# Attention scores with the low part of q against the high part of k alone, as two 64-row products, and the last head's query tiles in reverse order

## The chip, the cores and the metric

The kernel runs on one core of one Trainium2 chip. The metric is the device time of one execution in microseconds. A core has a matrix engine (TensorE, PE in the rows, with its weight loads as PEld), VectorE (DVE), ScalarE (ACT), GpSimd (POOL) and SyncE (SP), which issues the DMAs.

## The reference, cut to what matters

A decoder block over 16 learned meta tokens and 1024 positions of width 1024: a differential-attention branch and a gated-linear-attention branch, merged by gates, with a residual and an RMSNorm at the end. The change concerns the differential attention: 8 heads, each with two maps of head size 64.

```
def probs(q, k):
    s = einsum("bhqd,bhkd->bhqk", q, k) * 64 ** -0.5
    return softmax(where(k_pos <= q_pos, s, -inf))
p   = probs(q1, k1) - lam * probs(q2, k2)
o_a = einsum("bhqk,bhkv->bhqv", p, v)      # then RMSNorm, silu gate, w_branch_a
```

All is float32. The kernel splits each operand into a high part (the type fp32r, which the matrix engine takes in one pass) and a low part, the rest, and sums the products of the parts.

## The kernel before

The kernel runs in stages: normalise and transpose x, project it (a Strassen form for most weights), the linear-attention heads, then the attention stage, branch a, and the output projection. In every stage a small planner (class `Schedule`) is given operations with an engine, an estimated time, dependencies, buffers ("rings") and priorities. It simulates them once and so writes out a fixed order for each engine; on the chip an engine takes its instructions in that order.

In the attention stage a head has eight query tiles `t` of 128 rows, and each tile two maps `j`. A score tile `i` is one (tile, map). Query tile `qt` sees `nk` = 16 + 128 (`qt` + 1) keys, the meta keys first. The operands stand so that the parts are joined by the contraction over 128 rows: `q[:, 0]` holds the high part of q twice (rows 0 to 63 and 64 to 127), `q[:, 1]` the low part twice, and the tile `kk` the high part of k in rows 0 to 63 and the low part in rows 64 to 127. So `qh` times `kk` is high times high plus high times low (L1738), and `ql` times `kk` is low times high plus low times low (L1739). Then a product of an identity with a bf16 mask is added on the diagonal block (L1741). Tiles with `nk` over 512 are cut into two pieces of equal width in two PSUM banks; for `qt` 7 the 16 meta keys are done apart (L1750, L1751). Two score tiles fit at a time (ring "S", two buffers of two banks).

After a score tile come: the max on VectorE (L1767), the exp on ScalarE with its sum (L1779), for both maps the reciprocal (L1787), the scaling of the second map on GpSimd (L1791) and the combination on VectorE (L1796). For each pair `n` of query tiles `value(n)` transposes the combined p (L1852; the meta keys at L1831), splits it and multiplies it with v (L1873 for meta, L1879 to L1881), one pair after the other; then the norm (L1903), the gate (L1918, L1919), a split into high and low (L1935, L1939) and, except for the last head, a store to DRAM. The last head's results go into the place of a tile that branch b reads.

In the gaps PE gets the remaining v projection (L453 to L455) and branch b (L2021 to L2023 into `ps_y`). Branch a, the same lines into `ps_s`, follows and takes the banks of the scores.

The loads of `kk`, q (two halves of four query tiles, one buffer each), v (`va`, `vb`, one buffer each) and meta v (`vm`, three DMAs) are in SP's order. Those of heads 0 and 1 that come at the beginning are issued by `early(i)` of the stage before, in this order: k and first q half of head 0, second q half, k of head 1, v and meta v of head 0. `kk` has two buffers, so head h + 2 is loaded when head h has its last scores.

For the rows of other places: L427 to L429 are projection products, L564 and L589 those of the Strassen form, L1359 a product in the linear-attention heads over the 16 meta rows with plain F32 operands, which PE runs as two pieces, and L1511 a like one over 128 rows.

Of the kernel before, what the change touches and what calls it, by code (L numbers as in the profile page):

```python
# [10 lines left out]
F32 = mybir.dt.float32  # L11
# [9 lines left out]
P = 128  # L21
D = 1024
KC = D // P
NM = 16
# [141 lines left out]
def tile_hybrid_block(  # L166
# [1500 lines left out]
    with ExitStack() as es:  # L1667
# [26 lines left out]
        def load_q(h, hf):  # L1694
            def run():
                for j in range(2):
                    load_qj(A["pool"] if hf else sq, h, hf, j)

            loads["q", h, hf] = op("SP", 3.0 if h else 0.0, run if h else lambda: None, take=f"q{hf}", lat=3.0,
                                   prio=16 * h + 8 * hf)  # L1700

        def load_v(h):
            for i, (k, us) in enumerate((("va", 1.5), ("vb", 1.5), ("vm", 0.5))):
                run = (lambda i=i: load_vp(h, i)) if h else lambda: None
                st = tuple(vst[h // 2]) if h // 2 >= VA else ()
                loads[k, h] = op("SP", us if h else 0.0, run, st, take=k, lat=3.0, prio=16 * h + (8 if i == 1 else 4))
# [3 lines left out]
        step, stat = {}, {}  # L1710
# [5 lines left out]

        def scores(i):
            h, qt, j = i // 16, i % 16 // 2, i % 2
            nk = n_of(i // 2)
            big = nk > 1024  # L1720
            qh, ql, kk = qk(h, j, qt)
            sc = psS.tile([P, 2, 512], F32, name="ps_s", tag="s")
            extra = None
            if nk <= 512:
                pieces = [(0, nk, sc[:, 0, :nk])]
                k0, n, ps = 0, nk, sc[:, 0, :nk]
            elif not big:
                hn = nk // 2
                pieces = [(0, hn, sc[:, 0, :hn]), (hn, hn, sc[:, 1, :hn])]
                k0, n, ps = 0, nk, sc[:, :, :hn]  # L1730
            else:
                extra = tiles["mk", h][:, j]
                pieces = [(NM, 512, sc[:, 0]), (NM + 512, 512, sc[:, 1])]
                k0, n, ps = NM, 1024, sc[:, :, :]
            diag = nk - P
# [6 lines left out]
            step[i] = (k0, n, ps, extra)  # L1742

        def meta_scores(h):

            ms = psY.tile([P, 512], F32, name="ps_ms", tag="misc")[:, : 2 * NM]
            for j in range(2):
                qh, ql, kk = qk(h, j, 7)
                d = ms[:, NM * j : NM * (j + 1)]
                mm(d, qh, kk[:, :NM], start=True, stop=False)  # L1750
                mm(d, ql, kk[:, :NM], start=False, stop=True)  # L1751
            tiles["ms", h] = ms
# [18 lines left out]
        def expo(i):  # L1771
            k0, n, ps, extra = step.pop(i)
            t, j = i // 2, i % 2
            b = stat[t]["nm"][:, j : j + 1]
            pt = tiles["p", t, j] = s3.tile([P, T], F32, name=f"p{j}", tag=f"p{j}", bufs=sch.rings[f"p{j}"])
            dst = pt[:, k0 : k0 + n]
            if len(ps.shape) == 3:
                dst = dst.rearrange("p (a b) -> p a b", a=2)
            act(dst, ps, AF.Exp, bias=b, accum_out=stat[t]["sm"][:, j : j + 1])  # L1779
            if extra is not None:  # L1780
                act(pt[:, :NM], extra, AF.Exp, bias=b, accum_out=stat[t]["sm2"][:, j : j + 1])
# [7 lines left out]
        def second(t):  # L1789
            p2 = tiles["p", t, 1][:, : n_of(t)]  # L1790
            nc.gpsimd.tensor_scalar(p2, p2, stat[t]["r"][:, 1:2], nlam, ALU.mult, ALU.mult)  # L1791

        def both(t):

            p1, p2 = (tiles["p", t, j][:, : n_of(t)] for j in range(2))
            stt(p1, p1, stat[t]["r"][:, 0:1], p2, ALU.mult, ALU.add)  # L1796
            del stat[t], tiles["p", t, 1]

        def softmax(t):
            h, qt = t // 8, t % 8  # L1800
            nk = n_of(t)
            if qt == 7:
                ms = op("PE", 0.4, lambda: meta_scores(h), (S_[2 * t - 1],), take="misc", prio=2 * t - 3)
                mk = op("ACT", 0.09, lambda: meta_copy(h), (ms,), take="mk", use=(("misc", ms),), prio=2 * t - 3)
            for j in range(2):
# [3 lines left out]
                deps = (q, kk) + ((S_[i - 1],) if i else ()) + ((mk,) if qt == 7 else ())  # L1809
# [3 lines left out]
                M_[i] = op("DVE", dm, lambda i=i: vmax(i), (S_[i],) + ((mk,) if qt == 7 else ()),  # L1813
                           take="" if j else "sm", use=(("mk", mk),) if qt == 7 else (), prio=i + PR["M"])
                de = nk * 0.84e-3 + 0.23 + (0.3 if qt == 7 else 0)
                E_[i] = op("ACT", de, lambda i=i: expo(i), (M_[i],) + ((E_[i - 1],) if i else ()), take=f"p{j}",
                           use=(("S", S_[i]),) + ((("mk", mk),) if qt == 7 else ()), prio=i + PR["E"])
            b = 2 * t + 1
# [9 lines left out]
        def meta_t(n):  # L1828
            pv = psY.tile([P, 512], F32, name="ps_pm", tag="misc")[:NM, :256]
            for qi in range(2):  # L1830
                nc.tensor.transpose(pv[:, P * qi : P * (qi + 1)], tiles["p", 2 * n + qi, 0][:, :NM], ident)  # L1831
            val[n]["mv"] = pv

        def meta_hi(n):
            pm = val[n]["pm"] = pms[n % 2]
# [7 lines left out]
        def trans(n, b):  # L1843
            tp = psT.tile([P, 512], F32, name="ps_t", tag="t")
            blocks, o = [], 0
            for kb in (2 * b, 2 * b + 1):
                o0 = o
                for qi in range(2):
                    if kb > 2 * (n % 4) + qi:
                        continue  # L1850
                    p = tiles["p", 2 * n + qi, 0][:, NM + P * kb : NM + P * (kb + 1)]
# [69 lines left out]
        def out_parts(n):  # L1921
# [6 lines left out]
            if pq == 0:  # L1928
# [20 lines left out]
        def value(n):  # L1949
            h, pq = n // 4, n % 4  # L1950
            t0 = 4 * n + 3
# [7 lines left out]
            for b in range(pq + 1):  # L1959
# [9 lines left out]
                          (tl, v) + ((ml, vm) if first else (last,)) + ((A_[n - 1],) if first and n else ()),  # L1969
# [20 lines left out]
            else:  # L1990
                hi = op("ACT", 0.27, lambda: out_split_hi(n), (gt, *oops["b", h]) + tuple(oa_last[:1]), take="" if pq else f"o{h}",
# [33 lines left out]
        def branch(kind, i, order, bank, take, evac, w):  # L2025
# [4 lines left out]
            for n, (k, c) in enumerate(order):  # L2030
# [11 lines left out]
                prev = op("PE", mm3(512), run, (w["ops"][k // 4],) + src_deps(kind, k, c) + ((prev,) if prev else ()), take=t,  # L2042
# [48 lines left out]
        for t in range(8 * H):  # L2091
            softmax(t)
            if t % 2:
                value(t // 2)
# [50 lines left out]
        for i in range(KC):  # L2145
# [4 lines left out]
            ends = branch("a", i, order, bank_s if i < KC - 1 else bank_1, "S", evac_a, w)  # L2150
# [416 lines left out]
```

## Time and profile before

| | |
|---|---|
| median of 3 runs | 1374.7 us (1372.65 to 1375.21) |
| the profiled execution | 1372.48 us, span 1370.7 us |
| granted TensorE clock, mean | 0.995 |
| TensorE busy | 1320.3 us (96%), weight loads 1153.7 us (84%) |
| VectorE, ScalarE, GpSimd busy | 875.6, 748.7, 591.0 us |
| attention stage | about 861 to 1170 us |

The times of the trace count from the span's start. Matmuls overlap in their pipeline, so that their durations add up to more than the time they take; the distance from one to the next, or from end to end, says what one costs. Idle time is put down to what ended it ("<-"), "issue" being idle time for which the profile shows no wait.

### The profile page before, as it was taken

How to read it: one execution, taken by the hardware profiler on the slowest of the kernel's cores; microseconds unless marked ns; L12 is line 12 of the kernel's file. 1: busy time of each engine (PE TensorE's matmuls, PEld its weight loads, DVE VectorE, ACT ScalarE, POOL GpSimd, SP SyncE). 2: the span in 40 equal slices, each digit the busy share in tenths (PEclk: the TensorE clock that was granted, in tenths of full speed). 3: DMA queues.
4: the chain of work that ended last, by engine and by line, in shares of the span. 5: the costliest groups of instructions: out<-in, count | busy, mean ns of one | idle time of the engine just before them, and what ended most of it. 6: DMA issues, size and time to landing. Idle time of an engine off the chain costs nothing.

```text
span 1370.7 us, 22183 instructions
## 1 busy us (share of the span) xinstructions
PE 1320.3 (96%) x7736; PEld 1153.7 (84%) x7736; DVE 875.6 (64%) x1456; ACT 748.7 (55%) x1639; POOL 591.0 (43%) x598
## 2 busy tenths in 40 slices
PE   6999999999999999999999999899999999999897
PEld 5988889889888888888999999788888888778686
DVE  5845464555555444458778885677777778366874
ACT  7643332553566665664546554577777677321433
POOL 4113232452445323215455454447676665443534
PEclk9999999999999999999999999999999999999999
DMA  6226473324433333284734583788765653787232
GB/s 225 90 70 200 137 248 117 108 85 126 131 123 103 106 115 115 93 252 145 218 97 140 185 281 109 231 296 273 252 217 185 205 186 116 259 289 261 93 123 85
DMA packets 133696, 229.22 MB, mean 167 GB/s; under 512 B 14273, under 2 KB 60673, under 8 KB 133585
## 3 DMA queue, kind: packets, MB, share of 16 engines
q1 hardware_dynamic: 133216, 226.50, 50.0%
q0 software_dynamic: 368, 1.31, 0.3%
q8 instruction: 61, 1.00, 0.3%
q14 instruction: 51, 0.41, 0.1%
HBM read 143.55 MB, written 84.21 MB: 166 GB/s over the span
## 4 chain that ended last, share of the span: by engine, by line
PE 78%; DVE 8%; ACT 4%; DMA 4%; issue 3%; POOL 2%; SPq 0%; POOLq 0%; DVEq 0%; ACTq 0%
PE ps_st L564 28%; PE ps_st L589 6%; PE ps_proj L427 3%; PE ps_proj L428 3%; PE ps_proj L429 3%; PE ps_t L2361 2%; PE ps_s L2021 2%; PE ps_s L2022 2%; PE ps_s L2023 2%; PE ps_s L1738 2%; PE ps_l L1449 2%; PE ps_t L1852 2%; PE ps_s L1739 1%; PE ps_y L2021 1%; PE ps_y L2361 1%
## 5 line engine op out<-in xcount | busy, mean ns | idle before, releaser
L512 POOL TENSOR_TENSOR s<-w_raw 128x512 f32<-128x512 f32 x48 | 69.8, 1471 | 195.9 <-DMA w_raw<-in_w_col_dram 134.1
L564 PE MATMUL ps_st<-th,wh 128*128 128x512 f32 x352 | 137.0, 389 | 0.7 <-DVE u L578 0.7
L564 PE MATMUL ps_st<-tl,wh 128*128 128x512 f32 x352 | 136.9, 389 | 0.0
L564 PE MATMUL ps_st<-th,wl 128*128 128x512 f32 x352 | 136.9, 389 | 0.0
L247 DVE TENSOR_TENSOR wl<-s,wh 128x512 fp32r<-128x512 f32 x96 | 76.6, 798 | 62.5 <-ACT wh L246 62.4
L246 ACT CAST wh<-s 128x512 fp32r<-128x512 f32 x96 | 59.4, 619 | 103.2 <-PE ps_st L564 51.7
L1779 ACT ACTIVATE p<-ps_s,nm 128x272 f32<-128x272 f32 (+7 forms) x128 | 96.4, 756 | 27.9 <-DVE nm L1767 16.3
L1437 POOL TENSOR_TENSOR xl<-lg 128x256 f32<-128x256 f32 x112 | 79.8, 738 | 72.0 <-PE ps_l L1449 20.1
L1767 DVE TENSOR_REDUCE nm<-ps_s 128x1 f32<-128x272 f32 (+7 forms) x128 | 97.0, 766 | 20.7 <-PE ps_s L1741 16.5
L427 PE MATMUL ps_proj<-u_hi,w_hi 128*128 128x346 f32 (+3 forms) x320 | 104.0, 325 | 3.2 <-DVE cc L578 2.3
L564 PE MATMUL ps_st<-u_hi,wh 128*128 128x512 f32 x264 | 102.8, 389 | 1.0 <-issue 1.0
L564 PE MATMUL ps_st<-u_lo,wh 128*128 128x512 f32 x264 | 102.7, 389 | 0.0
L564 PE MATMUL ps_st<-u_hi,wl 128*128 128x512 f32 x264 | 102.7, 389 | 0.0
L428 PE MATMUL ps_proj<-u_lo,w_hi 128*128 128x346 f32 (+3 forms) x320 | 98.6, 308 | 2.6 <-DVE u_lo L756 2.5
L429 PE MATMUL ps_proj<-u_hi,w_lo 128*128 128x346 f32 (+3 forms) x320 | 97.8, 306 | 0.0
L246 ACT CAST wh<-w_raw 128x512 fp32r<-128x512 f32 x70 | 43.1, 616 | 94.0 <-PE ps_st L564 88.5
L247 DVE TENSOR_TENSOR wl<-w_raw,wh 128x512 fp32r<-128x512 f32 x70 | 60.9, 871 | 45.7 <-ACT wh L246 45.7
L1738 PE MATMUL ps_s<-kk,q 128*128 128x264 f32 (+7 forms) x208 | 74.3, 361 | 5.2 <-ACT p L1779 4.9
L564 PEld LDWEIGHTS ps_st<-th,wh 128*128 128x128 f32 x352 | 66.1, 188 | 14.8 <-ACT sg L290 1.1
L512 POOL TENSOR_TENSOR s<-w_raw,s 128x512 f32<-128x512 f32 x22 | 28.5, 1295 | 113.9 <-DVE wl L247 113.9
L564 PEld LDWEIGHTS ps_st<-th,wl 128*128 128x128 f32 x352 | 66.1, 188 | 13.7
L564 PEld LDWEIGHTS ps_st<-tl,wh 128*128 128x128 f32 x352 | 66.1, 188 | 13.6
(400 smaller groups left out, 4304.3 us busy)
## 6 DMA issues: line engine op xcount, KB each, us to landing
w_raw<-in_w_col_dram SPq DMA_DIRECT2D x54, 512.0 KB, 3.6
q<-d_q SPq DMA_DIRECT2D x32, 512.0 KB, 5.4
kk<-d_k SPq DMA_DIRECT2D x16, 520.0 KB, 6.6
d_g<-sg SPq DMA_DIRECT2D x32, 256.0 KB, 2.0
va<-d_v SPq DMA_DIRECT2D x16, 512.0 KB, 5.5
d_q<-qhi SPq DMA_DIRECT2D x24, 256.0 KB, 3.1
d_q<-qlo SPq DMA_DIRECT2D x24, 256.0 KB, 3.4
w_raw<-in_w_row_dram SPq DMA_DIRECT2D x12, 512.0 KB, 4.2
```

Source lines behind the costliest of these rows:

```text
L246: nc.scalar.copy(hi, raw)
L247: (eng or nc.vector).tensor_tensor(lo, raw, hi.bitcast(F32), ALU.subtract)
L427: mm(b["ps"], wh, rh, start=kc == 0, stop=False)
L428: mm(b["ps"], wh, rl, start=False, stop=False)
L429: mm(b["ps"], wl, rh, start=False, stop=kc == KC - 1)
L512: nc.gpsimd.tensor_tensor(r, x, y, op)
L564: mm(ps, w[:, k], x[k], start=start and k == 0 and i == 0, stop=k == KC // 2 - 1 and i == 2, skip_group_check=not start,)
L589: mm(ps[ti // 2][:, r], x[k][:, c], w[:, k % 2], start=start and k == i == 0 and ti % 2 == 0, stop=k == KC // 2 - 1 and i == 2 and ti % 2 ...
L1437: nc.gpsimd.tensor_tensor(ap(X["xl", li], o1, *to), x if e else ref, ref if e else x, ALU.subtract)
L1738: mm(pp, qh, kk[:, c0 : c0 + w], start=True, stop=False)
L1767: nc.vector.tensor_reduce(b, ps, AX.XY if len(ps.shape) == 3 else AX.X, ALU.max, negate=True)
L1779: act(dst, ps, AF.Exp, bias=b, accum_out=stat[t]["sm"][:, j : j + 1])
```

## The change

The scores of query tiles 3 to 7 take the low part of q against the high part of k alone. For that the columns of `kk` (and with them those of p) get a new order: the key blocks with even number, backwards, then the 16 meta columns at `KM` = 512, then the odd blocks. In the columns below `KM` the high part of k stands in rows 0 to 63, from `KM` on in rows 64 to 127. The keys of a query tile are one range around `KM`; a score tile has one piece below and one above it. `qh` meets both over 128 rows as before; `ql[:64]` meets the piece below and `ql[64:]` the piece above, each over 64 rows, into different banks. The product of the two low parts is dropped for these tiles. Tiles 0 to 2 keep one piece over 128 rows with both products. A load of `kk` becomes four DMAs for the even blocks and, for each part of k, one for the meta columns and one for the odd blocks.

The pairs of query tiles of the last head are taken in the order 6 and 7, 4 and 5, 2 and 3, 0 and 1; the priorities of its loads of q and v follow, and branch a waits for the last score and finds the last head's results in that order.

```diff
+    KM = 512
+    def kpos(kb):
+        return KM + NM + 64 * (kb - 1) if kb % 2 else KM - P - 64 * kb
     def load_kj(pool, h, j):
         t = QK["k", h, j] = pool.tile([P, T], F32R, name="kk", tag=f"kk{j}")
-        nc.sync.dma_start(t.bitcast(F32), d_k[2 * h + j].rearrange("e d t -> (e d) t"))
+        dst, src = t.bitcast(F32), d_k[2 * h + j]
+        for kb in range(0, 8, 2):
+            nc.sync.dma_start(dst[:, kpos(kb) : kpos(kb) + P], src.rearrange("e d t -> (e d) t")[:, NM + P * kb : NM + P * (kb + 1)])
+        for e in range(2):
+            r = slice(64 - 64 * e, 128 - 64 * e)
+            nc.sync.dma_start(dst[r, KM : KM + NM], src[e, :, :NM])
+            nc.sync.dma_start(dst[r, KM + NM :].rearrange("p (b c) -> p b c", c=P),
+                              src[e, :, NM:].rearrange("d (b o c) -> d b o c", o=2, c=P)[:, :, 1])
...
-                                   prio=16 * h + 8 * hf)
+                                   prio=16 * h + 8 * (hf ^ (h == H - 1)))
...
+        turns = list(range(4 * H - 4)) + [4 * H - 1 - k for k in range(4)]
+        place_of = {n: p for p, n in enumerate(turns)}
...
+        def first_key(t):
+            return KM - P * (t % 8 // 2 + 1)
         def scores(i):
...
-            for c0, w, pp in pieces:
-                has = c0 <= diag < c0 + w
-                mm(pp, qh, kk[:, c0 : c0 + w], start=True, stop=False)
-                mm(pp, ql, kk[:, c0 : c0 + w], start=False, stop=not has)
-                if has:
-                    mm(pp[:, diag - c0 : diag - c0 + P], identb, maskb[:, qt % 2], start=False, stop=True)
+                k1 = KM
+                if nk > 1024:
+                    extra = tiles["mk", h][:, j]
+                    k1 += NM
+                n1 = k0 + nk - k1
+                pa, pb = flat[:, k0:KM], flat[:, KM : KM + n1]
+                mm(pa, qh, kk[:, k0:KM], start=True, stop=False)
+                mm(pb, qh, kk[:, k1 : k1 + n1], start=True, stop=False)
+                mm(pa, ql[:64], kk[:64, k0:KM], start=False, stop=qt % 2 == 1)
+                mm(pb, ql[64:], kk[64:, k1 : k1 + n1], start=False, stop=qt % 2 == 0)
+                ps, sh = (sc[:, :, :] if extra is not None else flat[:, k0 : k0 + nk]), KM - k1
+            d = diag + (sh if diag > KM or nk <= 512 else 0)
+            mm(flat[:, d : d + P], identb, maskb[:, qt % 2], start=False, stop=True)
...
-                S_[i] = op("PE", 2 * nk * 0.417e-3 + 0.16, lambda i=i: scores(i), deps, take="S",
-                           use=((f"q{qt // 4}", q), ("kk", kk)), prio=i)
+                half_ = max(KM - first_key(t), first_key(t) + nk - KM) if nk > 512 else nk
+                S_[i] = op("PE", (nk + half_) * 0.417e-3 + 0.16, lambda i=i: scores(i), deps, take="S",
+                           use=((f"q{qt // 4}", q), ("kk", kk)), prio=p + j)
...
-                return tuple(oa_ops[4 * k + 2 * c : 4 * k + 2 * c + 2])
+                return tuple(oa_ops[4 * k + 2 - 2 * c : 4 * k + 4 - 2 * c])
...
-        for t in range(8 * H):
-            softmax(t)
-            if t % 2:
-                value(t // 2)
+        for n in turns:
+            softmax(2 * n)
+            softmax(2 * n + 1)
+            value(n)
...
-            ends = branch("a", i, order, bank_s if i < KC - 1 else bank_1, "S", evac_a, w)
+            ends = branch("a", i, order, bank_s if i < KC - 1 else bank_1, "S", evac_a, w,
+                          (S_[prev[0]],))
```

## Rows read from the trace of the kernel before

**Rows 1.** The page: busy time of TensorE, share of the span, instructions.

```profile
PE 1320.3 (96%) x7736; PEld 1153.7 (84%) x7736; DVE 875.6 (64%) x1456; ACT 748.7 (55%) x1639; POOL 591.0 (43%) x598
```

**Rows 2.** Busy time by stretch: attention stage; length, engines, granted clock, DMA.

```profile
861.00:1170.00 309.00, 298.66 (x1979) 255.17 (x1978) 239.16 (x428) 228.57 (x608) 188.78 (x231) 0.99 0.65 216
```

**Rows 3.** Waits of PE, 861 to 1170 us: total, times, longest.

```profile
PE ps_s L1738 <- ACT p L1779: 4.9, 7, 1.7
...
PE ps_pm L1831 <- DVE p L1796: 0.2, 1, 0.2
```

**Rows 4.** The chain that ended last, in time: start, length, what.

```profile
79.80 114.26 PE ps_st L564 x503
...
295.42 2.87 PE ps_st L589 x24
```

**Rows 5.** Timeline, a score tile of query tile 7: start, length, what.

```profile
885.64 0.39 PE L1738 MATMUL ps_s<-kk,q 128*128 128x512 f32 x1
...
886.57 0.10 PEld L1741 LDWEIGHTS <-identb 128*128 128x128 bf16 x1 [0.27 <-issue]
```

**Rows 6.** Timeline, two 16-row products (rows*columns of weights first), PE and PEld.

```profile
606.16 0.32 PE L429 MATMUL ps_proj<-u_hi,w_lo 128*128 128x346 f32 x1
606.41 0.18 PEld L1359 LDWEIGHTS ps_d<-gvm,kmt 16*128 16x128 f32 x1 [0.21 <-issue]
606.41 0.29 PEld L1359 LDWEIGHTS ps_d<-gvm,kmt 16*128 16x128 f32 x2 [0.21 <-issue]
606.41 0.48 PE L1359 MATMUL ps_d<-gvm,kmt 16*128 16x256 f32 x1
606.73 0.37 PE L1359 MATMUL ps_d<-gvm,kmt 16*128 16x256 f32 x1
607.03 0.19 PEld L427 LDWEIGHTS ps_proj<-u_hi,w_hi 128*128 128x128 f32 x1 [0.33 <-issue]
607.03 0.43 PE L427 MATMUL ps_proj<-u_hi,w_hi 128*128 128x346 f32 x1
```

**Rows 7.** Line 1359: shortest, median, longest duration in ns, first and last start.

```profile
L1359 PE MATMUL ps_d<-gvm,kmt x8: 374/426/478, 606.4 to 795.3; 16*128 16x256 f32 x8
```

**Rows 8.** Timeline, a like product over 128 rows.

```profile
614.83 0.32 PE L429 MATMUL ps_proj<-u_hi,w_lo 128*128 128x346 f32 x1
614.99 0.59 PE L1511 MATMUL ps_d<-gv,kt 128*128 128x256 f32 x2
```

**Rows 9.** Timeline, the first product with meta v.

```profile
875.46 0.36 PE L1873 MATMUL ps_v<-pm,vm 80*128 80x256 f32 x1
875.65 0.29 PE L1879 MATMUL ps_v<-th,va 128*128 128x256 f32 x1
```

**Rows 10.** Line 1068, issues of kk: ns of one (shortest, median, longest), first and last start.

```profile
L1068 SPq DMA_DIRECT2D kk<-d_k x16: 320/464/1319, 809.4 to 1088.0; - x16
```

**Rows 11.** DMA issues of the whole run: count, KB each, median us to landing.

```profile
q<-d_q SPq DMA_DIRECT2D x32, 512.0 KB, 5.4
kk<-d_k SPq DMA_DIRECT2D x16, 520.0 KB, 6.6
...
vm<-d_v SPq DMA_DIRECT2D x24, 8.0 KB, 4.8
```

**Rows 12.** Timeline of SP's issues at the start of the stage.

```profile
864.82 0.94 SPq L1068 DMA_DIRECT2D kk<-d_k  x2
...
868.11 0.46 SPq L1655 DMA_DIRECT2D vm<-d_v  x1
```

**Rows 13.** Timeline at the change from head 6 to 7: SP, then PE.

```profile
1125.11 0.39 SPq L1073 DMA_DIRECT2D q<-d_q  x1
1126.45 0.23 PE L1738 MATMUL ps_s<-kk,q 128*128 128x144 f32 x1
```

**Rows 14.** Waits of PE, 1166 to 1300 us: total, times, longest.

```profile
PE ps_s L2021 <- DVE g L2125: 1.2, 1, 1.2
...
PE ps_y L2021 <- DVE gl L2067: 1.0, 2, 0.7
...
PE ps_v L1873 <- ACT oa L1885: 0.4, 1, 0.4
```

More of the change, by code (lines that the diff above doesn't have):

```diff
@@ L1705, in load_v, with turn_of @@
                 st = tuple(vst[h // 2]) if h // 2 >= VA else ()
-                loads[k, h] = op("SP", us if h else 0.0, run, st, take=k, lat=3.0, prio=16 * h + (8 if i == 1 else 4))
+                loads[k, h] = op("SP", us if h else 0.0, run, st, take=k, lat=3.0, prio=16 * h + (8 if i == 1 and h < H - 1 else 4))
         S_, M_, E_, FB_, A_ = {}, {}, {}, {}, {}
-        step, stat = {}, {}
+        turns = list(range(4 * H - 4)) + [4 * H - 1 - k for k in range(4)]
+        place_of = {n: p for p, n in enumerate(turns)}
+        def turn_of(t):
+            return 2 * place_of[t // 2] + t % 2
+        step, stat, prev = {}, {}, []
         def qk(h, j, qt):
@@ new lines, in scores @@
+                mm(o, ql, kk[:, k0 : k0 + nk], start=False, stop=False)
+                ps, sh = o, -k0
+            else:
+                k1 = KM
[9 more added lines that the diff above has]
+                ps, sh = (sc[:, :, :] if extra is not None else flat[:, k0 : k0 + nk]), KM - k1
@@ L1749, in meta_scores @@
                 d = ms[:, NM * j : NM * (j + 1)]
-                mm(d, qh, kk[:, :NM], start=True, stop=False)
-                mm(d, ql, kk[:, :NM], start=False, stop=True)
+                mm(d, qh, kk[:, KM : KM + NM], start=True, stop=False)
+                mm(d, ql, kk[:, KM : KM + NM], start=False, stop=True)
             tiles["ms", h] = ms
@@ L1789, in second @@
         def second(t):
-            p2 = tiles["p", t, 1][:, : n_of(t)]
+            p2 = tiles["p", t, 1][:, first_key(t) : first_key(t) + n_of(t)]
             nc.gpsimd.tensor_scalar(p2, p2, stat[t]["r"][:, 1:2], nlam, ALU.mult, ALU.mult)
         def both(t):
-            p1, p2 = (tiles["p", t, j][:, : n_of(t)] for j in range(2))
+            p1, p2 = (tiles["p", t, j][:, first_key(t) : first_key(t) + n_of(t)] for j in range(2))
             stt(p1, p1, stat[t]["r"][:, 0:1], p2, ALU.mult, ALU.add)
@@ L1830, in meta_t @@
             for qi in range(2):
[L1831 removed]
+                nc.tensor.transpose(pv[:, P * qi : P * (qi + 1)], tiles["p", 2 * n + qi, 0][:, KM : KM + NM], ident)
             val[n]["mv"] = pv
         def meta_hi(n):
[L1835 removed]
+            pm = val[n]["pm"] = pms[place_of[n] % 2]
             for r in (0, 64):
@@ L1850, in trans @@
                         continue
-                    p = tiles["p", 2 * n + qi, 0][:, NM + P * kb : NM + P * (kb + 1)]
+                    p = tiles["p", 2 * n + qi, 0][:, kpos(kb) : kpos(kb) + P]
                     nc.tensor.transpose(tp[:, o : o + P], p, ident)
@@ L1927, in out_parts @@
                 return
-            if pq == 0:
+            if ("o", "a", h) not in tiles:
                 tiles["o", "a", h] = otile(h)
@@ L1968, in value @@
                 last = op("PE", 0.71 + 0.12 * first, lambda b=b: apply_v(n, b),
-                          (tl, v) + ((ml, vm) if first else (last,)) + ((A_[n - 1],) if first and n else ()),
+                          (tl, v) + ((ml, vm) if first else (last,)) + ((A_[turns[pn - 1]],) if first and n else ()),
                           take="V" if first else "",
@@ L1990, in value @@
             else:
-                hi = op("ACT", 0.27, lambda: out_split_hi(n), (gt, *oops["b", h]) + tuple(oa_last[:1]), take="" if pq else f"o{h}",
+                hi = op("ACT", 0.27, lambda: out_split_hi(n), (gt, *oops["b", h]) + tuple(oa_last[:1]), take="" if oa_last else f"o{h}",
                         use=(("oa", oc),), prio=x + PR["OH"])
@@ L2023, in parts3, with branch @@
             mm(dst, w[1], x[0], start=False, stop=last)
-        def branch(kind, i, order, bank, take, evac, w):
+        def branch(kind, i, order, bank, take, evac, w, after=()):
             prev, first, last = None, {}, {}
@@ L2041, in branch @@
                 t = take if n == 0 or ((take == "Y" or order[1][1] == 0) and c not in first) else ""
-                prev = op("PE", mm3(512), run, (w["ops"][k // 4],) + src_deps(kind, k, c) + ((prev,) if prev else ()), take=t,
+                prev = op("PE", mm3(512), run, (w["ops"][k // 4],) + src_deps(kind, k, c) + ((prev,) if prev else after), take=t,
                           use=(w["own"], (f"o{k}", oops[kind, k][0])), prio=jobs.seq)
```

45 lines of the change are left out of this document (21 added, 24 removed).

## The prediction

> **What bounds the kernel now.** The page comes first: TensorE (PE) is busy for 96% of the span [rows 1]. A busy share proves little, so the table of stretches is next: the change lies in 861 to 1170 us, the attention stage, where PE is busy 298.7 of 309.0 us at a granted clock of 0.99 (the higher level, 2.4 GHz); VectorE has 239.2, ScalarE 228.6, and the DMA engines a share of 0.65 [rows 2]. The waits of PE there add up to 9.7 us in eight lines, half of it scores that wait for an exp to free their bank [rows 3]. PE runs a fixed order and is full: a microsecond of PE time added in this stage is a microsecond of the end, less what those waits give back.
>
> What a matmul costs is read from the chain, not from busy time: 503 products of 512 columns follow one another in 114.26 us, 0.227 us each, and 24 of 256 columns in 2.87 us, 0.120 us each [rows 4]. So a product costs 0.42 ns a column plus 0.012 us; its weight load is hidden behind the product before it. In a score tile only the load of the bf16 mask is not: its idle time is marked "issue", it starts 0.93 us after the tile does, when the four products of 0.23 us are through [rows 5].
>
> **The scores, term by term.** Query tiles 3 to 7 of a head (80 score tiles over 8 heads and two maps) lose two low products over 128 rows and get two over 64 rows. Columns before: 2x264, 2x328, 2x392, 2x456, 2x512; after: 256+272, 384+272, 384+400, 512+400, 512+512. Tiles 0 to 2, the high products, the mask, the max and the exp keep their sizes. The low products of the five tiles cost 0.246 + 0.300 + 0.353 + 0.407 + 0.454 = 1.76 us a map now [rows 4], 28.2 us over 16 maps. If the two 64-row products ran side by side and nothing else changed, the longer one would remain: 0.126 + 0.173 + 0.180 + 0.227 + 0.227 = 0.93 us, a gain of 0.83 us a map, 13.2 us in all.
>
> Against it speaks one kind of place in the trace: two products over 16 rows between products over 128 [rows 6]. The last 128-row product ends at 606.16 + 0.32 = 606.48, the first 16-row piece at 606.89, the second at 607.10. A piece adds 0.21; so going in cost 0.41 - 0.21 = 0.20 us. The load was not fetched early, it starts at 606.41. Coming out, the load starts at 607.03 and its product ends at 607.46, 0.36 after the last piece, where 346 columns take 0.16: again 0.20. Of this 0.11 is the load and 0.09 is more than the load. (The second 16-row load starts 0.11 after the first: 0.29 together, 0.18 alone.) The trace has four such places; their eight pieces last 374 to 478 ns, the first of each pair with the load in it [rows 7]. The cause is not the plain F32 type: two such pieces over 128 rows end at 615.58, 0.43 after the product before them, so 0.21 each and nothing for going in [rows 8]. Nor is it any change of rows: leaving a product over 80 rows, the next one ends 0.12 later, as usual [rows 9].
>
> I take that price for 64 rows. In: 0.20. Out: the mask's load is not fetched early today either, so only the 0.09 is new. The second 64-row product starts 0.11 after the first, behind its load. Per tile: 0.29 + max(first, 0.11 + second), at 0.42 ns a column: 0.514, 0.514, 0.568, 0.568, 0.615 = 2.78 us a map against 1.76: +1.02, times 16 = **+16.3 us**. That is 0.20 a tile, so it would be nought if the switch cost 0.09 in place of 0.29.
>
> The Trainium skill has a rule for the switch (TensorEngine Tiling (Array Packing), Key Properties): changing the tiling mode drains the engine. It says nothing of loads. By a drain alone, the 0.09 above each way with all loads fetched early, the sum would be 0.18 + the longer product, 1.77 us a map: +0.2 us, no change. The rows have the load on top, both ways, and I go by them.
>
> Bounds. Both loads at once: 0.29 + the longer product, 2.32 us a map, **+9.0**. No overlap at all: 1.70 + 1.45 = 3.15, **+22.2**. No price and full overlap: **-13.2**. Between them I take +16.3, since the only two neighbouring loads inside a narrow group of this size stand 0.11 apart.
>
> **What takes some of it back.** With PE 5% slower (16.3 of 309), ScalarE and VectorE catch up and the 9.7 us of waits [rows 3] shrink: -4 (0 to -9.7).
>
> **The k loads.** One DMA of 520 KB becomes eight, with rows of 512 bytes and less; 16 issues a head for 2. An issue takes 0.464 us in the median [rows 10], so the 14 new ones hold SP for 6.5 us. From head 2 on they start a head ahead (309 / 8 = 39 us) and land in some 7 [rows 11], so they are hidden: 0 (up to +3, if loads of z, q or v behind them come late). Head 0's own k is issued at 809.4, 50 us before the first score [rows 10]: nothing. Head 1's is not covered so well: its issues at 864.82 stand ahead of head 0's v and meta v. The third meta v goes out at 868.11 [rows 12] and lands 4.8 later in the median [rows 11], 872.9; PE takes it first at 875.46 [rows 9]. 6.5 us later it is 4 us late, and the first value products hold up the transposes behind them in PE's order. Part is regained from the waits that follow: +2 (0 to +5).
>
> **The last head in reverse.** Its first pair needs the second half of q, whose buffer is free only after the last scores of head 6. The second of its two loads goes out at 1125.11 and takes 5.4 [rows 11, 13], the first score of head 7 runs at 1126.45: some 4 us late for the second map, with branch b's products standing in the same place: 0 (up to +3). At the other end the last pair is short instead of long. After 1166 us PE waits 4.6 us in five lines, of which 2.6 are at lines 2021 and 1873, which the reversal could shorten [rows 14]. But the splits of the last head still wait for branch b to release their place, so two gate chains still follow it: -1 (-4 to +2). That branch a's first product now waits for the last score costs nothing: its sums take the scores' banks, which come free after them anyway.
>
> **Sum.** +16.3 - 4 + 0 + 2 + 0 - 1 = +13.3. The profiled execution took 1372.5 us (span 1370.7 and 1.8 around it): 1385.8. The median of the runs, 1374.7, lies 2.2 above it; on that footing **1388**.
>
> **The rivals**, in median time; 0.2% (2.7 us) is about what a measurement of this kernel can tell from no change.
> A, the forecast: switch paid both ways, loads one after the other, products overlap: 1388. 38%.
> B, both loads at once: +9.0 for +16.3, so +6: 1381. For it: the loads fill different rows; against: rows 6. 27%. The Trainium skill is on this side (TensorE: Matmul & The Clock Gate, Part 3): products in different row groups start some 4 ns apart, and a load overlaps work of another row group. No run so far shows two groups at work.
> C, no overlap: +22.2, so +19.2: 1394. 12%.
> D, the other side: 64-row products are no switch, as 80 rows are none, their loads are fetched early, and they overlap: -13.2 + 2 - 1 = -12: 1362. It decides from a switch of less than 0.09 us a tile on. For it: 16 rows were seen to pay, not 64. Against: the four places pay alike, whatever follows them. 15%.
> E, the change does not do what it says: no switch, no overlap, the two products in the old time: +1: 1376. 8%.
>
> The likeliest alone reaches from 1382 to 1394. The range takes in B, C and E with the bounds of the smaller terms and leaves D out: 1371 to 1399. Faster by over 0.2%: D, 16% with a little of E. Within: most of E and the low end of B, 10%. Slower: 74%.
>
> **What would show it.** In the profile after: the load of the first 64-row product starting about 0.09 after the product before it has streamed, marked idle for "issue"; the ends of the pair 0.11 apart in the 512-column tile (A), level (B), or 0.21 (C); a tile of query 7 from its start to the mask's load 1.1 us long in place of 0.93; the attention stage 12 to 15 us longer at the same number of PE instructions; the first product with meta v some 4 us late, behind DMA. It would be wrong if the 64-row loads are fetched during the high products (D), or if PE idles for ScalarE, DMA or q in sums over 10 us: then the layout or the order sets the end, and not the array.

## The result and the profile after

The changed kernel takes 1408.9 us (median of 4 runs, 1407.77 to 1409.84) against 1373.7 (4 runs) of the kernel before: ratio 1.0257, 95% interval 1.0239 to 1.0276. That is 35 us slower, beyond the forecast (1388) and its range (1371 to 1399). Below, "so many us slower" is always the difference of a kernel's median to that of the kernel before in the same session, with the ratio's interval beside it.

The page of the kernel after, TensorE's line; it answers to [rows 1]:

```profile
PE 1340.1 (95%) x7736; PEld 1149.8 (82%) x7736; DVE 870.8 (62%) x1456; ACT 751.4 (53%) x1639; POOL 583.9 (41%) x598
```

TensorE (PE) is busier by 20 us in a span longer by 37. The attention stage now ends about 1211 us, and its stretch reads, against [rows 2], with five pieces of it in the lines under it (stretch, length, busy time and count of PE, PEld, DVE, ACT, POOL, granted clock, DMA share, GB/s):

```profile
861.00:1211.00 350.00, 324.31 (x2023) 256.16 (x2021) 237.40 (x429) 229.49 (x601) 180.25 (x224) 0.97 0.66 210
882.00:886.00 4.00, 3.97 (x16) 3.33 (x17) 0.72 (x1) 1.17 (x3) 0.61 (x1) 0.50 0.85 225
886.00:890.00 4.00, 4.00 (x18) 2.78 (x17) 1.85 (x4) 2.00 (x4) 1.39 (x2) 0.62 0.97 323
934.00:938.00 4.00, 4.00 (x22) 3.02 (x22) 1.28 (x2) 2.92 (x8) 1.92 (x3) 0.65 1.02 363
979.00:983.00 4.00, 3.73 (x16) 3.11 (x16) 0.66 (x1) 1.62 (x5) 0.61 (x1) 0.50 0.97 361
983.00:987.00 4.00, 3.54 (x16) 2.10 (x15) 2.12 (x5) 2.14 (x5) 1.45 (x2) 0.80 0.99 385
```

PE idles for 26 us there, where it idled for 10, and in places it runs at the lower clock level (0.50 is 1.2 GHz). The waits of PE in the stage, kernel after, against [rows 3]:

```profile
PE ps_v L1910 <- DMA va<-d_v: 8.4, 3, 5.0
PE ps_v L1904 <- DMA vm<-d_v: 5.7, 1, 5.7
PE ps_s L1751 <- ACT p L1806: 3.2, 3, 1.8
```

Two lines are new: 14.1 us for v and meta v. What made those loads late stands in the chain that ended last, followed through this stretch (start, length, what):

```profile
870.07 0.59 SPq L1081
...
876.39 0.37 SPq L1669
876.81 0.42 SPq L1669
877.27 4.63 DMA vm<-d_v
882.03 0.55 PE ps_v L1904
...
965.83 1.21 SPq L1077
...
974.13 0.60 SPq L1081
974.83 4.39 DMA va<-d_v
979.27 0.58 PE ps_v L1910
```

Lines 1077, 1080 and 1081 are the new issues of `kk`. The chain runs through SyncE's queue (SP), issue after issue, then through one load of v, and back to PE. At the start of the stage SP reads, against [rows 12]:

```profile
865.12 1.89 SPq L1077 DMA_DIRECT2D kk<-d_k  x4
...
874.57 0.60 SPq L1081 DMA_DIRECT2D kk<-d_k  x1
875.21 1.08 SPq L1666 DMA_DIRECT2D va<-d_v  x2
876.39 2.69 SPq L1669 DMA_DIRECT2D vm<-d_v  x6
```

Sixteen issues take 10.1 us, from 865.12 to 875.21, where two took 0.94 [rows 12]; in 1.4 us of them SP waits for a load of q that is still under way. The first product with meta v starts at 882.03 in place of 875.46 [rows 9]. Heads 1 and 2 are alike: the last product that reads `va` of the head before ends at 920.1 and 964.9, SP is then at the k issues (917.63 to 927.51 and 965.35 to 974.73), and the next `va` goes out behind them at 928.77 and 974.83. Those two loads make 8.1 of the 8.4 us.

The scores themselves, a tile of query tile 7 in the kernel after, against [rows 5]:

```profile
897.13 0.39 PE L1762 MATMUL ps_s<-kk,q 128*128 128x512 f32 x1
...
897.68 0.18 PEld L1764 LDWEIGHTS ps_s<-kk,q 64*128 64x128 f32 x1 [0.36 <-issue]
897.68 0.50 PE L1764 MATMUL ps_s<-kk,q 64*128 64x512 f32 x1
897.68 0.18 PEld L1765 LDWEIGHTS ps_s<-kk,q 64*128 64x128 f32 x1
897.68 0.50 PE L1765 MATMUL ps_s<-kk,q 64*128 64x512 f32 x1
898.12 0.10 PEld L1768 LDWEIGHTS <-identb 128*128 128x128 bf16 x1 [0.25 <-issue]
```

The first 64-row load is not fetched early; both loads start in the same 0.01 us, and both products end together. From the tile's start to the mask's load it is 0.99 us, 0.93 before [rows 5]. Taken over all tiles of a size in both traces, the median of that distance grows by 0.17, 0.15, 0.13, 0.11 and 0.03 us for query tiles 3 to 7: 0.58 a map, 9.3 us over 16 maps.

### The profile page after: what moved, and what is told of

It reads as the page before. It is cut to its first block, busy times and chain, and to the rows that moved or that the text cites. A ratio compares the mean times of both kernels' runs of the same rounds, so it can differ in the third digit from the quotient of the medians.

```text
span 1408.1 us, 22323 instructions
## 1 busy us (share of the span) xinstructions
PE 1340.1 (95%) x7736; PEld 1149.8 (82%) x7736; DVE 870.8 (62%) x1456; ACT 751.4 (53%) x1639; POOL 583.9 (41%) x598
## 2 busy tenths in 40 slices
DMA packets 151872, 229.24 MB, mean 163 GB/s; under 512 B 18112, under 2 KB 80896, under 8 KB 151760
## 4 chain that ended last, share of the span: by engine, by line
PE 79%; DVE 8%; DMA 5%; ACT 3%; issue 3%; SPq 2%; POOL 1%; POOLq 0%; DVEq 0%; ACTq 0%
PE ps_st L564 28%; PE ps_st L589 6%; PE ps_proj L428 3%; PE ps_proj L427 3%; PE ps_proj L429 2%; PE ps_s L2053 2%; PE ps_s L2054 2%; PE ps_s L2055 2%; PE ps_t L2394 2%; PE ps_y L2053 2%; PE ps_s L1764 2%; PE ps_t L1883 2%; PE ps_y L2055 2%; PE ps_l L1463 2%; PE ps_y L2054 2%
## 5 line engine op out<-in xcount | busy, mean ns | idle before, releaser
L247 DVE TENSOR_TENSOR wl<-s,wh 128x512 fp32r<-128x512 f32 x96 | 76.4, 796 | 64.0 <-ACT wh L246 63.9
L1451 POOL TENSOR_TENSOR xl<-lg 128x256 f32<-128x256 f32 x112 | 80.1, 739 | 71.8 <-PE ps_l L1463 20.1
L1818 POOL TENSOR_SCALAR p<-p,r,nlam 128x144 f32<-128x144 f32 (+3 forms) x64 | 54.4, 850 | 57.6 <-DVE r L1814 49.9
L1897 DVE TENSOR_TENSOR tl<-ps_t,th 128x512 fp32r<-128x512 f32 (+1 forms) x80 | 50.7, 634 | 40.6 <-ACT th L1892 40.0
```

What stands on the lines that cost most here:

```text
L247: (eng or nc.vector).tensor_tensor(lo, raw, hi.bitcast(F32), ALU.subtract)
L1451: nc.gpsimd.tensor_tensor(ap(X["xl", li], o1, *to), x if e else ref, ref if e else x, ALU.subtract)
```

## The experiments

Theory after these views: three prices that add up, the switch of the scores (some 10 us), the k loads in SP's queue (15 to 20), the reversal (3 to 8). Rivals: all of it is the switch; the loads are hidden; the reversal is harmless.

| run | what it is | slower than before, us | ratio, 95% |
|---|---|---|---|
| the change | the whole of it | 35.2 | 1.0239 to 1.0276 |
| switch_only | kernel before, low products over 64 rows, one behind the other | 15.3 | 1.0096 to 1.0126 |
| no_rev | the change, last head in its old order | 32.2 | 1.0221 to 1.0252 |
| k_loads_only | the change, old order, whole low products | 18.7 | 1.0119 to 1.0172 |
| rev_only | kernel before, last head reversed | 1.3 | 1.0000 to 1.0021 |
| v_first | the change, k loads behind the v loads | 25.7 | 1.0161 to 1.0205 |
| lean | the change, 10 issues a head in place of 16 | 18.3 | 1.0091 to 1.0160 |
| one_load | the change, one load a k tile (keys in the wrong columns) | 11.8 | 1.0059 to 1.0094 |
| lean_vfirst | both of lean and v_first | 12.4 | 1.0064 to 1.0104 |
| nr_lean_vfirst | lean_vfirst, last head in its old order | 15.7 | 1.0077 to 1.0127 |
| pair_lean_vfirst | lean_vfirst, one switch for two maps | 23.5 | 1.0155 to 1.0192 |
| pair_best | the same, old order, query tile 3 whole | 22.9 | 1.0146 to 1.0181 |
| split_k | v first at the start, later k issues free one by one | 90.1 | 1.0632 to 1.0674 |
| start_only | v first at the start alone | 37.2 | 1.0250 to 1.0303 |
| v_first_10 | v_first, the planner told 10 us | 25.3 | 1.0151 to 1.0208 |
| v_first_2x5 | v_first, the planner told two steps of 5 us | 30.4 | 1.0201 to 1.0243 |

The median of the kernel before itself lies between 1373.1 and 1376.1 us in the six sessions (the rows stand in their order: the change; two groups of four; three; split_k; three), so that a difference of 3 us between rows of different sessions settles nothing.

**The parts alone.** The switch without its gain (kernel before; high products first, then the low ones):

```diff
-                mm(pp, ql, kk[:, c0 : c0 + w], start=False, stop=not has)
+            for c0, w, pp in pieces:
+                has = c0 <= diag < c0 + w
+                r = 64 if nk > 512 else P
+                mm(pp, ql[:r], kk[:r, c0 : c0 + w], start=False, stop=not has)
```

> The kernel before with one edit: in the tiles of qt 3 to 7 (80 in all) the two low products of a tile stand behind its two high ones and use 64 rows of q and k, both the same 64, so the row group is switched in and out once a tile, nothing overlaps and no column is saved. Layout, loads and order are those before; the upper 64 rows of low q are left out of the scores. Theory (three separable causes: the switch, the k loads, the reversal): a switch costs 0.20 us in and 0.09 out, 80 x 0.29 = 23 us of TensorE, less some 2 to 8 that the waits of the stage take in: 15 to 21 us slower than before, and no wait for a load of v or k. Rival (the switch alone makes the 35 us of the change, which got 13 back by overlapping): 35 + 13 = about 48 us slower. Second rival (the switch is hidden under the waits for the other engines): under 5 us slower.

15.3 us, at the lower end of what the theory had. Its tile of query tile 7, timeline:

```profile
888.31 0.63 PE L1738 MATMUL ps_s<-kk,q 128*128 128x512 f32 x2
888.87 0.29 PEld L1742 LDWEIGHTS ps_s<-kk,q 64*128 64x128 f32 x2 [0.36 <-issue]
888.87 0.73 PE L1742 MATMUL ps_s<-kk,q 64*128 64x512 f32 x2
889.53 0.10 PEld L1744 LDWEIGHTS <-identb 128*128 128x128 bf16 x1 [0.36 <-issue]
```

1.22 us to the mask's load where [rows 5] show 0.93: the switch costs 0.29 in and out, with no other change (0.26 to 0.29 by the medians of the five sizes). The two loads into the same 64 rows take 0.29 together. The changed kernel's 0.99 is then 0.93 + 0.29 less one product of 512 columns, 0.23.

The change without the reversal, the deadlines put back with it:

```diff
-        turns = list(range(4 * H - 4)) + [4 * H - 1 - k for k in range(4)]
+        turns = list(range(4 * H))
```

> The changed kernel with the pairs of the last head in their old order (its deadlines for q, v and the gate's sources put back too); the 64-row products, the key layout and the k loads stay. Theory: the switch (about 10) and the loads (15 to 20) stay, so 25 to 31 us slower than before, that is 4 to 10 faster than the changed kernel (35 slower than before). Rival (the reversal is harmless or a gain): 35 to 39 us slower than before.

32.2: between the two theories, 3 us under the change, whose interval overlaps with its own. The loads alone (that kernel, with the low products whole):

```diff
-                mm(pa, ql[:64], kk[:64, k0:KM], ...)
-                mm(pb, ql[64:], kk[64:, k1 : k1 + n1], ...)
+                mm(pa, ql, kk[:, k0:KM], ...)
+                mm(pb, ql, kk[:, k1 : k1 + n1], ...)
```

> As the run without the reversal, and both low products of a tile again over 128 rows, with the planner's old price for a score tile: only the key layout and the eight loads for each k tile in place of one are left of the change. Theory: the 16 issues for a head take about 10 us of SyncE's queue, the v loads behind them land late, and PE waits for v as in the changed kernel (5.7, 3 and 5 us): 15 to 20 us slower than before. Rival (the loads lie beside other work, as the prediction had it): under 5 us slower.

18.7, as the theory had it, with no 64-row product in the kernel. Its longest wait of PE is that for meta v:

```profile
PE ps_v L1904 <- DMA vm<-d_v: 6.6, 1, 6.6
```

The loads are no cheap part of the change but the dearest. The reversal alone, on the kernel before:

> The kernel before with only the last head's pairs of query tiles in reverse (deadlines of its q, v and gate sources moved with them, and branch a behind the last score, as in the change); scores, layout and k loads as before. Theory (the tail's waits of the changed kernel, 3.6 us for the gate's load and the 4 to 5 us by which the tail there is longer, come of the reversal): 3 to 8 us slower than before. Rival (the tail as predicted): between 4 us faster and 1 us slower.

1.3: at the rival's upper end (a little over it), so that the theory's reading of the tail falls; the waits of the changed kernel's tail are not the reversal's alone.

**What it is about the loads.** Order, number of issues, or traffic:

```diff
 v_first: # the k loads behind v
-            elif i == 2:                  # early(): load_kj of head 1
+            elif i == 5:                  # v and meta v of head 0 at 2 to 4
...
-            loads["k", h] = op("SP", ..., take="kk", ...)
+            loads["k", h] = op("SP", ..., tuple(loads[x, h - 1] for x in ("va", "vb", "vm")) if h > 1 else (), take="kk", ...)
 lean:    # one DMA for the four even blocks
-        for kb in range(0, 8, 2):
-            nc.sync.dma_start(dst[:, kpos(kb) : kpos(kb) + P], ...)
+        ev = dst[:, kpos(0) : kpos(0) + P]
+        nc.sync.dma_start(bass.AP(ev.tensor, ev.offset, [ev.ap[0], [-P, 4], [1, P]]), ...)
 one_load: # one DMA in place of the eight, keys in their old places
-        for kb in range(0, 8, 2):
...
+        nc.sync.dma_start(dst, src.rearrange("e d t -> (e d) t"))
```

> The changed kernel with one thing moved: the k loads of a head (from head 1 on) are issued behind the v loads (va, vb, vm) of the head before, not ahead of them; the sixteen issues and their bytes stay. Theory 1 (the issues stand in SyncE's queue ahead of the v loads, and these land late): PE's 14.1 us of waits for vm and va go, so about 35 - 14 = 21 us slower than before, 16 to 24 with what hangs on it. Theory 2 (the transfers themselves, 18,000 packets more, slow all others) and theory 3 (SyncE's time for the issues, whatever their order): 30 us or more slower.

> The changed kernel with the four loads of the even key blocks of a k tile made one load (same bytes to the same places, the blocks taken with a negative step): 10 issues a head in place of 16, same packets, same order. Theories 1 and 3 (SyncE's issues): 10/16 of the 10 us of issues stay, v lands 3 to 4 us earlier, and of the waits for v in three heads 8 to 11 us go: 23 to 28 us slower than before. Theory 2 (the transfers): 33 to 37 us slower, as the changed kernel.

> The changed kernel with one load for each k tile in the order of the keys in DRAM, as before; the products stay as changed, so the scores meet the keys in the wrong columns. It gives the whole price of the k loads in the changed kernel. If the parts add up (the loads 20, as the run of the loads alone had it): 35 - 20 = 15 us slower than before, 12 to 17, with no wait for v. If the parts hide each other (the loads' price is the greater for the longer scores, or the smaller): under 10 or over 20.

> Both edits: 10 issues a head, and behind the v loads of the head before. Theory 1: nothing of the loads is left on the path, 12 to 18 us slower than before, within 3 us of the run with one load for each tile. Theory 2: 30 or more; theory 3: 23 to 28, as with 10 issues alone.

One load leaves 11.8 us and no wait for v, so the loads cost 35.2 - 11.8 = 23.4. It is not the traffic: ten issues move the same bytes to the same places, in 151,103 packets against 151,872 (133,696 before), and give back 17, more than theories 1 and 3 had for them; with v in front all 23 come back. So it is the issues that cost. v first alone gives back 9.5: at 25.7 it lies between theory 1 (16 to 24) and the others (30 or more). One place where the rest stayed is seen in the timeline of that run:

```profile
890.11 0.72 POOL L1949 TENSOR_TENSOR za<-za,sq 128x256 f32<-128x256 f32 x1 [9.36 <-DMA za<-d_za]
890.91 0.72 POOL L1950 TENSOR_TENSOR oa<-oa,za 128x256 f32<-128x256 f32 x1
891.62 1.00 POOL L1818 TENSOR_SCALAR p<-p,r,nlam 128x784 f32<-128x784 f32 x1
...
892.66 1.48 DVE L1823 SCALAR_TENSOR_TENSOR p<-p,r,p 128x784 f32<-128x784 f32 x1 [6.02 <-POOL p L1818]
...
894.19 0.28 PE L1862 MATMUL ps_pm<-ident,p 128*16 128x128 f32 x1 [3.95 <-DVE p L1823]
```

With v ahead, the gate's load of z still stands behind the k issues: the first goes out at 882.84, in the kernel before at 876.73. GpSimd waits 9.36 us for z (4.69 before, where PE's waits for p are 0.2 in all [rows 3]), the next tile's p stands behind that gate in GpSimd's order, and PE loses 3.95. The late load is another; the wait is the same kind.

Ten issues won more than their share, since a wait is what other work leaves of a delay: the three long waits for v (5.7, 3.1 and 5.0 us) become two short ones, and what stays of the 14.1 is little. Waits of PE in the run with ten issues (lean):

```profile
PE ps_v L1905 <- DMA vm<-d_v: 2.1, 1, 2.1
PE ps_v L1911 <- DMA va<-d_v: 1.4, 1, 1.4
```

So 10.6 us of waits went and 17 us of time. The rest is the clock: after each wait in the changed kernel the granted clock stands at 0.50 to 0.80 for some microseconds (stretches above). By those five rows it takes 3.97 x 0.50 + 4.00 x 0.38 + 4.00 x 0.35 + 3.73 x 0.50 + 3.54 x 0.20 = 7.5 us. 14.1 of waits and 7.5 of clock make 21.6 of the 23.4. The Trainium skill describes this (TensorE: Matmul & The Clock Gate, HAM oscillation — how this bites in real kernels): a wait for a DMA sends the clock down, and the work after it starts slow. The rows agree: behind the wait of 5.7 us that ends at 882.03 the granted clock is 0.50 in the next 4 us.

The same can be added up for whole traces, from 861 us to the end in windows of 4 us: the busy time of PE times its granted clock (work), its idle time, and the rest of its busy time (lost to the clock), in us. The work of rev_only, whose products are those of the kernel before, adds up to 484.8, so that 2 us between two traces mean nothing.

| run | work | idle | lost to the clock |
|---|---|---|---|
| before | 482.4 | 23.9 | 3.3 |
| the change | 490.3 | 41.4 | 15.4 |
| one_load | 490.1 | 27.5 | 4.3 |
| lean | 491.6 | 31.1 | 6.4 |
| lean_vfirst | 490.1 | 27.5 | 3.9 |
| switch_only | 503.5 | 20.1 | 2.9 |
| pair_lean_vfirst | 482.7 | 43.4 | 9.1 |

Between the change and one_load the work is the same; 13.9 us of idle time and 11.1 of clock make the 25.2 by which the two spans differ; between the change and lean they are 10.3 and 9.0.

**The start alone, and the planner.** The term that the prediction gave a number to, and whether a plan that knows SP's time would help (the planner holds 3 us for a head's k loads):

```diff
 start_only: only early() of v_first
 v_first_10: v_first, and
-            loads["k", h] = op("SP", 3.0 if h > 1 else 0.0, ...)
+            loads["k", h] = op("SP", 10.0 if h > 1 else 0.0, ...)
 v_first_2x5: two steps of 5.0, one for each map
 split_k:    early() of v_first, and from head 2 on 16 steps of 0.6, free to stand anywhere
```

> The changed kernel with one move at the start of the attention stage alone: the 16 k issues of head 1 stand behind va, vb and vm of head 0; all later heads as in the change. It sizes the term that the prediction put at 2 us (0 to 5). If the wait for vm (5.7 us by the waits, 6.1 by the gaps of TensorE) is that term's whole price: 5 to 8 us faster than the changed kernel, 27 to 30 slower than before. Rival (what is won is given back to the next load in the queue): 32 to 36 slower.

37.2, the rival's side, 1 us over its range: PE no longer waits for meta v, but the wait for p takes its place (GpSimd waits 10.00 us for z there), and the later waits for va (9.2 us) stay:

```profile
PE ps_v L1910 <- DMA va<-d_v: 9.2, 2, 5.0
PE ps_pm L1862 <- DVE p L1823: 4.6, 1, 4.6
```

> The changed kernel with the k loads of head 1 behind the v loads of head 0, and from head 2 on each of the 16 issues its own step for the planner, at 0.6 us, in place of one step of 3 us for all: the planner then knows SyncE's time and may put other loads (v, za, q) between them. Issues, bytes and products stay. Theory (an unbroken run of 10 us, planned as 3, holds up whatever stands behind it: v in the changed kernel, the gate's za load where v went ahead): nearly all of the loads' 23 us comes back, 12 to 18 us slower than before. Rival (SyncE's time for 16 issues a head is the price in any order): 23 to 30 us slower.

90.1, a miss for both, and it says nothing on the question. The planner let other steps on SP go ahead of the free ones, so that the first mask product of head 2 starts at 1007.9 us (947.6 in the changed kernel), and filled PE with branch b meanwhile. Line 2069 (branch b's first product into `ps_y`; first and last start) ends 99 us earlier than in the changed kernel (2053), and the heads after that have nothing to fill their gaps with (from 1100 to 1200 us PE is busy for 76.4 us, at a granted clock of 0.77):

```profile
L2069 PE MATMUL ps_y<-u_hi,w_hi x128: 392/396/505, 942.0 to 1100.3; 128*128 128x512 f32 x128
```

```profile
L2053 PE MATMUL ps_y<-u_hi,w_hi x128: 390/398/506, 948.3 to 1199.3; 128*128 128x512 f32 x128
```

> The run with the k loads behind the v loads, with the planner told 10 us for a head's k loads in place of 3; the run of 16 issues stays unbroken. Theory 4 (the plan is 7 us wrong about SyncE in each head, so that the order of all engines behind it no longer fits the real times): 12 to 18 us slower than before. Theory 5 (the unbroken run is the price: za, q and the stores behind it land late, whatever the plan holds): 23 to 28 slower, as with v first alone (25.7).

> As the run before it, with the 16 issues as two steps of 5 us, one for each map's k tile, between which the planner may place other loads. Theory 4: 12 to 18 us slower than before, as told 10 us at once. Theory 5: 17 to 22, between v first (25.7) and 10 issues with v first (12.4), since the longest run is then 5 us.

25.3 and 30.4: the wrong figure in the plan is not the cause (theory 4 falls), and theory 5 had v_first_10 right but not the two shorter runs, which were to take 17 to 22. With 10 us in the plan PE is busy for 3.6 us more in the first half of the stage and for 5.2 less in the second. Stretches of v_first and, below, of v_first_10 (columns as above):

```profile
861.00:1050.00 189.00, 172.53 (x1095) 138.52 (x1094) 125.29 (x226) 120.49 (x323) 97.46 (x123) 0.95 0.72 223
1050.00:1210.00 160.00, 155.47 (x960) 121.49 (x961) 119.74 (x210) 113.26 (x292) 88.12 (x109) 1.00 0.64 208
```

```profile
861.00:1050.00 189.00, 176.08 (x1129) 141.80 (x1130) 123.92 (x227) 120.02 (x320) 100.01 (x124) 0.98 0.74 232
1050.00:1210.00 160.00, 150.32 (x927) 116.75 (x926) 118.02 (x209) 113.74 (x293) 83.85 (x105) 0.98 0.63 201
```

A new plan moves the filler too, and how much of the 30.4 is that was not separated. So why v first alone keeps 13 us more than v first with ten issues is shown at the one place above and otherwise open. Issuing the k loads from another engine's queue was not tried.

**Can it pay?** With the loads out of the way, the switch is left. The old order of the last head; one switch for both maps of a tile; and that with query tile 3 left whole:

```diff
 pair_lean_vfirst:
-                mm(pa, ql[:64], kk[:64, k0:KM], ...)
-                mm(pb, ql[64:], kk[64:, k1 : k1 + n1], ...)
+                def low():
+                    mm(pa, ql[:64], kk[:64, k0:KM], ...)
+                    mm(pb, ql[64:], kk[64:, k1 : k1 + n1], ...)
+                lows.append(low)
...
+            masks.append(lambda: mm(..., identb, maskb[:, qt % 2], ...))
...
+            if nk <= 512 or j:          # pair_best: qt <= 3 or j
+                for x in lows + masks:
+                    x()
```

> The run with both edits to the k loads (10 issues a head, behind the v loads), with the last head's pairs in their old order. What is left of the change is then the 64-row products alone. Theory (a switch of 0.29 us a tile less the columns saved: 9 us over 80 tiles; the reversal 1 to 3): 9 to 11 us slower than before. Rival (the reversal costs nothing once the loads are out of the way): 12 us or more, as with the reversal.

> The run with both edits to the k loads, and one switch for two maps: in the tiles of qt 3 to 7 the high products of map 0, the high products of map 1, then the four low products of 64 rows, then both masks. Theory (the price of the scores is that of the switches): 40 of 80 go, 40 x 0.29 = 11.6 us, so between 1 us faster and 4 us slower than before. Rival (both score buffers are taken until the pair is done, so that PE waits for the maximum and the exponential of the tile before): the gain is eaten, 8 to 20 us slower than before.

> As the run with one switch for two maps, in the old order of the last head's pairs, and with whole low products of 128 rows for qt 3, whose tile saves least. By the tile times of the changed kernel (each map of qt 4 to 7 took 0.135, 0.123, 0.081 and 0.053 us more than before; half of a switch of 0.29 is 0.145): 16 x (0.010 + 0.022 + 0.064 + 0.092) = 3 us faster than before, 0 to 4 faster. Rival (buffers): 5 us or more slower.

15.7, with a spread of 9 us over four runs (1385.8 to 1395.0): no gain from the old order here. The shared switch loses 11 us where it should have won 11.6: at 23.5 it lies beyond even the rival's 20, and pair_best, at 22.9, is on the rival's side too. Waits of PE of the kernel with one switch for two maps, and below it the same wait without it (lean_vfirst):

```profile
PE ps_s L1764 <- ACT p L1817: 14.7, 10, 6.1
```

```profile
PE ps_s L1763 <- ACT p L1807: 0.5, 2, 0.2
```

Both score buffers belong to one pair, whose max and exp can start only when its second map is through, and PE waits for the exp of the tile before. The switches saved do show in PE's work (table above: 482.7 against 490.1), and 15.9 us of idle time and 5.2 of clock take more than that. But 482.7 is what the kernel before has (482.4): by this estimate the pairs would about break even, were there no waits. No version of the 64-row products tried here reaches the kernel before.

## Why the prediction was wrong

The side was right (74% on slower), the size was not: +13.3 forecast, +35 measured. The prediction's own sign of being wrong came true: PE idles for DMA in a sum over 10 us (14.1). Of its other signs, query tile 7's tile takes 0.99 us and not 1.1, meta v is 6.6 us late and not 4, and the stage is 41 us longer and not 12 to 15.

**The step that failed: the k loads.** It read "so they are hidden: 0 (up to +3, if loads of z, q or v behind them come late)" and, for head 1's, "+2 (0 to +5)". Measured: 23.4 us for both. For the later heads it asked when k itself would land, and k was in time; what stood behind its issues was late. For head 1 it did name what happened (meta v late behind the issues), and only the size was off. Three things were mis-sized. The later heads, costed at nothing, have no slack for v: `va` has one buffer, which the last pair of the head before must leave first, SP is at the k issues when it does, and the 8.4 us of waits for va are in heads past the start. A wait was costed at its own length, without the clock behind it: 7.5 us by the five rows. And the issues take 10.1 us at the start (8.7 without SP's wait for the load of q), not 2 x 0.464 + 6.5 = 7.4. The start's term cannot be measured by taking its wait away, since the next load in the queue then waits (start_only).

**The scores.** The price of the switch was right to 0.01 us: 0.29 a tile (switch_only). The loads "one after the other" were wrong: the two start together. The Trainium skill's rule (TensorE: Matmul & The Clock Gate, Part 3), by which a load overlaps work of another row group, agrees with that. The pair in [rows 6] from which the 0.11 was taken are loads for two pieces of one product, into the same rows, and so are those of switch_only, which again take 0.29 together; different rows had not been seen. The tile of query tile 7 grew by 0.06, and rival B gives 0.29 + 0.227 - 0.454 = 0.063. So B's +9.0 replaces +16.3 (it leaves out the 0.012 us that a product costs beside its columns; with it 1.45 + 0.93 - 1.76 = 0.62 a map, +10.0). The runs show 11.8 - 1.3 = 10.5 (one_load less rev_only), the tiles of the trace 9.3, the work of PE 7.9 (table above).

**The -4 from shrinking waits** did not come in the change: the waits of PE in the stage of lean_vfirst, all lines added, are 10.1 us, against 9.7 before [rows 3]. Filler moves with the plan, and the waits with it. It did come in switch_only, where only the scores take longer: PE's idle time falls from 23.9 to 20.1 us. That the forecast's +16.3 - 4 = 12.3 lies near the 10.5 is luck: one term was too dear and the other did not come.

**The reversal**, -1 (-4 to +2): 1.3 slower alone, 3 slower in the change, 3 faster with the loads mended, the last two with overlapping intervals. Within 3 us of nothing; its sign is not settled.

**Sum**: 10.5 of scores + 23.4 of loads + 1.3 = 35.2, by construction, since the first two are differences of runs. Two things stand apart from it: idle time and clock of the traces make the 25.2 us by which the spans of the change and one_load differ, and the loads without the 64-row products cost 18.7. That they cost 5 more in the changed kernel was not followed up; it may be noise, as the interval of k_loads_only reaches up to 1.0172, 23.7 us.

## What to carry to other kernels

When one load becomes many, cost the issues where they stand in their queue and ask for each load behind them what its first reader has to spare; a load into a buffer that exists once, as `va`, cannot go out before that buffer's last reader is done. A wait on TensorE that is long enough to drop the clock costs half as much again here or more (7.5 on 14.1 us by the five rows, 11.1 on 13.9 over the span), and a wait taken away at one place can return at the next load in the queue (wholly in start_only, in part in v_first) unless the issues get fewer. Narrow products in separate row groups do run side by side, but a switch of 0.29 us is worth some 700 columns at 0.42 ns, more than the 512 that one tile can save.

## What the runs showed that was not expected

- Two weight loads into different row groups of 64 start in the same 0.01 us and take 0.18 each, where two 16-row pieces, both in the same rows, started 0.11 apart [rows 6].
- Issues on SyncE are not negligible beside their transfers: 16 take 10.1 us, while each of the two loads that they replace lands 6.6 us after its issue [rows 11]. The Trainium skill (DMA: Bandwidth & Descriptors, Issuing engines are not separate DMA queues) calls the time to initiate a DMA usually small relative to the DMA. One by one that is so here (medians 0.43 to 0.60 us an issue, 2.4 to 2.8 us to landing); for sixteen in a row it is not, and the measurement decides.
- A load with a negative step over four blocks costs about one issue (0.61 us in lean_vfirst, 256 KB, 5.0 us to landing):

```profile
L1077 SPq DMA_DIRECT2D kk<-d_k x16: 594/610/647, 809.0 to 1106.1; - x16
...
kk<-d_k SPq DMA_DIRECT2D x14, 256.0 KB, 5.0
```
